# Nine raw buffers, 44 gating column tiles in the first chunk, DMAs on ScalarE's queue, later partial sums

## The chip, the core and the metric

The kernel runs on one core of a Trainium2 chip. The metric is the device time of one execution in microseconds. Before the change three runs took 3028.86 to 3030.75 us, with a median of 3030.44 us.

## What is computed

One layer of a diffusion backbone on a stream of 256 latent tokens with 256 context tokens as a prefix, width D = 4096, all in float32. Cut to what matters:

```python
mod   = silu(c) @ w_ada + b_ada             # shift, scale, gate (4096 each)
mod_c = silu(c_ctx) @ w_ada[:, :2*D] + ...  # shift, scale for the context
h  = rmsnorm(x, g) * (1 + scale) + shift    # 256 x 4096
hc = rmsnorm(ctx, g) * (1 + scale_c) + shift_c
xa, xb, ga, gb = split(h @ w_in)            # 4 x 4096 columns
xa_c = hc @ w_in[:, :4096]
ya = rglru_branch(xa, xa_c, ...)            # conv, gates, scans both ways
yb = pool_branch(xb, w_pool, ...)           # means over windows 2, 4, 8, 16
mixed = concat(ya * silu(ga), yb * silu(gb))
x = x + gate * (mixed @ w_out)
return rmsnorm(x, g_final)
```

The matrices are read once each, and they are most of what is moved: w_ada is 4096 x 12288, w_in 4096 x 16384, w_out 8192 x 4096.

## The kernel before

**Layout.** All activations lie transposed: features on the 128 partitions, tokens along the free axis. A tile of x holds 128 features of the 256 latent and the 256 context tokens (128 x 512), so D is 32 k-tiles. Every weight load is a raw tile of 128 x 1024 float32 (512 KB), taken from the pool of RAWB = 6 buffers and issued by SP (`load_raw`, line 92). `load_w` (line 97) splits it in two parts of lower precision: ACT casts raw to hi (line 101), and lo = raw - hi is made by DVE, or by POOL where the caller asks for it (line 103). The hi pool has 4 buffers, the lo pool 3. A product of float32 values is then three matmuls: hi x hi, hi x lo of the activation, and lo x hi.

**Stages.** In the head (to about 60 us) all 32 x tiles are loaded once for the sum of squares, and the modulation of the first chunk is made. Then comes the chunk stage (to about 900 us): the 32 k-tiles are taken in nine chunks of CHUNKS = (2, 4, 4, 4, 4, 4, 4, 4, 2).

- In chunk c, `xa_units` (line 338) multiplies the xa columns of w_in with the hc tiles of the chunk. A unit is one raw tile, which is two column tiles of 128 for a chunk of four k-tiles: 2 x 4 x 3 = 24 matmuls (lines 351 to 353) of 128 x 512 each, 16 units a chunk. The result of each column tile is in a PSUM tile, of which `mm_tile` has four; ACT copies three of four out to `part` (line 359) and POOL adds them to acc (line 360), DVE adds the fourth (line 362). lo is made by POOL here.
- Beside it, `ada_units` (line 228) makes shift and scale of the next chunk. Its 32 raw tiles of w_ss are not multiplied by PE but by DVE, which adds them up on 128 partitions (line 218); the last addition writes the four tiles fin (line 224). `rows` (line 261) then sums fin over partitions with matmuls against 0/1 columns (line 242; the program has four in the group, the trace counts eight), and `cols` turns the rows into columns (line 197).
- From these `prep_h` (line 301) makes the hc tiles of the next chunk: POOL multiplies x by rstd (line 305), ACT and DVE do the rest. `load_x` (line 317) fetches the x tile again.
- In the first chunk `ahead_units` (line 372) also multiplies the first two k-tiles of AHEAD = 28 of the 48 blocks of two column tiles that the later stage needs (56 column tiles; 12 matmuls of 128 x 256 a block, lines 384 to 386). `spill_ahead` (line 391) writes them to memory, seven a chunk, in chunks 1 to 4. `gated_units` fetches them back and adds them.

From about 900 us to 2300 us the pooling and gate columns follow (`block_units`, lines 618 and 619: 128 x 512 and 128 x 256 matmuls, lo made by DVE), with the scans between them; blocks that were begun ahead start at their third k-tile. The last stage, to 3008 us, is the output product in 16 blocks of 16 units; `out_evac` (line 752) loads the x tile of the residual (xr) when a block ends, adds it, and stores the first ten results to memory (line 775) until the final normalization.

**What sets the order.** The program is a list of events, and each engine runs its instructions in the order of a tile scheduler that takes them from that list. `run` (line 106) issues loads ahead: LOOK = 4 weight tiles and LOOK_A = 2 w_ss or w_gate tiles before their use. `spread` lays one list evenly among another. In chunk c the side list is: the w_ss units of chunk c + 1 that are left, `rows`, `cols`, and the `prep_h` calls; the w_ss units of chunk c + 2 that are already started are put in four pieces by LAGS = (0, 2, 5, 7, 10): two tenths before `rows`, three tenths between `rows` and `cols`, two behind `cols` and three behind three of the prep_h calls. Spills and x loads of the chunk are spread over the first 0.6 of the xa units.

Every DMA carries one of eight semaphores (DMAHW0 to 7), and before it starts it waits until the DMA that last used this semaphore has ended. The wait stands in the program of the engine that issues the DMA, and what follows it on that engine follows the wait.

Of the kernel before, what the change touches and what calls it, by code (L numbers as in the profile page):

```python
# [22 lines left out]
GATE_FROM, GATE_END = 0.9, 0.99  # L23
SPILL_Y = 10
EPS = 1e-6
POOL_ADDS = 3
EARLY = 4
NPREP = 3
LAGS = (0, 2, 5, 7, 10)
LRU_SPAN = 91  # L30
RAWB, HIB, LOB = 6, 4, 3
LOOK = 4
LOOK_A = 2
X_STEP = 2
SHARES = (16, 4, 0, 0, 0, 0, 0, 0, 0)
CHUNKS = (2, 4, 4, 4, 4, 4, 4, 4, 2)
AHEAD = 28
AHEAD_FROM = 48 - AHEAD
SPILLS = 7
W = 1024  # L40
# [25 lines left out]
def block_kernel(ctx, tc, xc, cvec, vecs, consts, w_ss, w_gate, w_xa, w_lat0, w_lat2, w_lat, w_pool, w_rec, w_out, out):  # L66
# [3 lines left out]
    cpool = ctx.enter_context(tc.tile_pool(name="consts", bufs=1))  # L70
    spool = ctx.enter_context(tc.tile_pool(name="slots", bufs=68))
    tpool = ctx.enter_context(tc.tile_pool(name="temps", bufs=14))
# [24 lines left out]
    def load_w(src, eng=None):  # L97
        raw = load_raw(src)
        width = src.shape[-1]
        hi = hip.tile([P, W], F32R, name="hi", tag="hi")[:, :width]  # L100
        act.copy(out=hi, in_=raw)  # L101
        lo = lop.tile([P, W], F32R, name="lo", tag="lo")[:, :width]
        (eng or dve).tensor_tensor(out=lo, in0=raw, in1=hi.bitcast(F32), op=SUB)  # L103
        return hi, lo

    def run(events):
# [194 lines left out]
    def prep_h(k):  # L301
        def f():
            x = xt[k]
            if k >= CHUNKS[0]:
                nc.gpsimd.tensor_tensor(out=x, in0=x, in1=rstd, op=MUL)
            h = mm_tile()
            for v in range(2):
                cut = slice(v * T, (v + 1) * T)
                act.activation(out=h[:, cut], in_=x[:, cut], func=AF.Identity, scale=colA[:, k, v:v + 1],
                               bias=colB[:, k, v:v + 1])  # L310
            hi, lo = temp("hhi", F32R), temp("hlo", F32R)
            split(hi, lo, h)
            hc[k] = (hi, lo)
            xt[k] = None
        return S_(f)

    def load_x(k):
        def f():
            xt[k] = slot("x")
            nc.sync.dma_start(out=xt[k], in_=xc[k])  # L320
        return S_(f)
# [16 lines left out]
    def xa_units(c):  # L338
# [3 lines left out]
        def unit(i):  # L342
            def f(w):
                hi, lo = (t.rearrange("p (k m) -> p k m", k=n) for t in w)
                for j in range(per):
# [26 lines left out]
    def ahead_units():  # L372
        def unit(i):
            def f(w):
                hi, lo = (t.rearrange("p (b k m) -> p b k m", b=2, k=2) for t in w)
                for b in range(2):
# [14 lines left out]
    def spill_ahead(blk):  # L391
        def f():
            nc.sync.dma_start(out=ahead_sp[blk], in_=ahead[blk])
            ahead[blk] = None
# [357 lines left out]
    def out_evac(blk):  # L752
        def f(j, ps):
            ct = 2 * blk + j
            if j == 0:
                xr = temp("xr")
                nc.sync.dma_start(out=xr.rearrange("p (k t) -> p k t", k=2),
                                  in_=xc[ct:ct + 2, :, 0:T].rearrange("k p t -> p k t"))
                ys.append(xr)
            y = ys[blk][:, j * T:(j + 1) * T]  # L760
# [13 lines left out]
            if j == 1 and blk < SPILL_Y:  # L774
                nc.sync.dma_start(out=y_sp[blk], in_=ys[blk])
        return f

    def warm_sqrt():
        t = temp("warm")[:, 0:1]
        act.activation(out=t, in_=ones[:, 0:1], func=AF.Sqrt)  # L780

    events += [make_mix(n) for n in range(4)] + [S_(warm_sqrt)]
    main = [block_units([w_out[blk, i] for i in range(16)], mix, out_evac(blk)) for blk in range(16)]
    pair = [u for two in zip(main[0], main[1]) for u in two]
    main = spread(pair, [make_mix(n) for n in range(4, 32)], 0.0, 28 / 32) + [u for m in main[2:] for u in m]
# [101 lines left out]
```

## Time and profile before

| | |
|---|---|
| median of three runs | 3030.44 us |
| the profiled execution | 3034.39 us, span 3032.6 us |
| mean granted clock of TensorE | 0.985 |
| bytes moved by DMA | 701 MB, 231 GB/s over the span |

The profile is one execution. A line for a stretch gives the busy time of PE (matmul), PEld (weight load), DVE, ACT and POOL, the clock that was granted to TensorE (1.00 is 2.4 GHz, 0.50 is 1.2 GHz) and the use of the 16 DMA engines. A line of waits gives the instruction that waited, what it waited for, the time in all, the number of times and the longest. SPq and ACTq are the queues in which an engine issues its DMAs.

### The profile page before, as it was taken

What the parts mean: (1) busy time and instruction counts of PE and PEld (TensorE: products, weight loads), DVE (VectorE), ACT (ScalarE), POOL (GpSimd) and SP (SyncE); (2) the same over time, 40 slices, a digit from 0 to 9 for tenths busy, and PEclk for the clock granted to TensorE, in tenths of its full rate; (3) what the DMA queues carried; (4) which work ended last, traced back from release to release, by engine and by line L of the source; (5) the groups of instructions that cost most, each with busy time, mean ns of one, the idle gap of its engine ahead of it and who ended that gap; (6) DMA issues with size and microseconds to landing.
All of it is one profiled execution on the core that took longest, in us unless ns stands there. A gap on an engine that the chain in (4) does not pass through costs nothing.

```text
span 3032.6 us, 40790 instructions
## 1 busy us (share of the span) xinstructions
PE 2898.6 (96%) x15032; PEld 2409.5 (79%) x15032; DVE 2232.4 (74%) x2723; ACT 1574.1 (52%) x2183; POOL 590.0 (19%) x348
## 2 busy tenths in 40 slices
PE   6997889899999999999999999999999999999997
PEld 3775667678778888888888888888888888788886
DVE  5787887888656778887777877778997766665445
ACT  4544334334434666766667766767663443333432
POOL 2566677687760000000000000000000000000000
PEclk9998999999999999999999999999999999999998
DMA  8889877788636555555556666666888988786664
GB/s 321 297 289 312 282 256 230 245 283 272 203 103 201 184 161 175 178 175 176 175 184 194 192 193 198 206 202 228 323 291 299 329 288 296 262 296 217 192 190 148
DMA packets 214968, 700.99 MB, mean 231 GB/s; under 512 B 23536, under 2 KB 31856, under 8 KB 214768
## 3 DMA queue, kind: packets, MB, share of 16 engines
q1 hardware_dynamic: 214768, 698.39, 69.7%
q8 instruction: 117, 1.92, 0.3%
q14 instruction: 83, 0.68, 0.1%
HBM read 675.75 MB, written 22.54 MB: 230 GB/s over the span
## 4 chain that ended last, share of the span: by engine, by line
PE 73%; DMA 12%; DVE 9%; issue 3%; POOL 2%; ACT 2%; SPq 0%; DVEq 0%; POOLq 0%; ACTq 0%
PE mm L618 34%; PE mm L619 17%; DMA raw<-in_w_gate 6%; PE mm L351 4%; DVE wide L218 4%; PE mm L352 4%; PE mm L353 4%; DMA raw<-in_w_ss 4%; PE wide L527 2%; PE wide L528 2%; PE wide L529 2%; DVE lo L103 2%; PE mm L242 1%; DMA x<-in_xc 1%; POOL lo L103 1%
## 5 line engine op out<-in xcount | busy, mean ns | idle before, releaser
L101 ACT CAST hi<-raw 128x1024 fp32r<-128x1024 f32 (+1 forms) x846 | 872.0, 1035 | 990.1 <-PE mm L618 539.8
L103 DVE TENSOR_TENSOR lo<-raw,hi 128x1024 fp32r<-128x1024 f32 (+1 forms) x704 | 840.6, 1200 | 369.8 <-PE mm L619 230.3
L618 PE MATMUL mm<-hT,hi 128*128 128x512 f32 x2960 | 1047.2, 398 | 0.0
L218 DVE SCALAR_TENSOR_TENSOR wide<-raw,sc,wide 128x1024 f32<-128x1024 f32 (+1 forms) x592 | 698.5, 1230 | 231.2 <-DMA raw<-in_w_ss 121.5
L619 PE MATMUL mm<-hT,lo 128*128 128x256 f32 x2960 | 831.3, 281 | 0.2 <-DVE lo L103 0.2
L618 PE MATMUL mm<-mix,hi 128*128 128x512 f32 x2048 | 723.8, 398 | 0.0
L618 PEld LDWEIGHTS mm<-hT,hi 128*128 128x128 f32 x2960 | 556.2, 188 | 138.9 <-ACT mix L134 0.9
L619 PE MATMUL mm<-mix,lo 128*128 128x256 f32 x2048 | 578.0, 282 | 13.4 <-DVE lo L103 13.2
L619 PEld LDWEIGHTS mm<-hT,lo 128*128 128x128 f32 x2960 | 559.1, 189 | 1.8 <-DVE lo L103 0.5
L618 PEld LDWEIGHTS mm<-mix,hi 128*128 128x128 f32 x2048 | 385.2, 188 | 94.6 <-ACT hi L101 1.7
L351 PE MATMUL mm<-hhi,hi 128*128 128x512 f32 x1024 | 403.1, 395 | 16.7 <-ACT hhi L134 7.4
L352 PE MATMUL mm<-hlo,hi 128*128 128x512 f32 x1024 | 401.0, 392 | 4.9 <-DVE hlo L135 4.9
L619 PEld LDWEIGHTS mm<-mix,lo 128*128 128x128 f32 x2048 | 387.4, 189 | 22.1 <-DVE lo L103 21.8
L353 PE MATMUL mm<-hhi,lo 128*128 128x512 f32 x1024 | 400.2, 391 | 0.0
L103 POOL TENSOR_TENSOR lo<-raw,hi 128x1024 fp32r<-128x1024 f32 x142 | 340.7, 2400 | 192.2 <-ACT hi L101 61.0
L351 PEld LDWEIGHTS mm<-hhi,hi 128*128 128x128 f32 x1024 | 193.0, 189 | 70.1 <-DVE acc L362 9.9
L360 POOL TENSOR_TENSOR acc<-acc,part 128x512 f32<-128x512 f32 x168 | 215.4, 1293 | 114.2 <-ACT part L359 114.0
L352 PEld LDWEIGHTS mm<-hlo,hi 128*128 128x128 f32 x1024 | 193.3, 189 | 46.9 <-DVE hlo L135 7.7
L353 PEld LDWEIGHTS mm<-hhi,lo 128*128 128x128 f32 x1024 | 193.2, 189 | 40.6
L359 ACT COPY part<-mm 128x512 f32<-128x512 f32 x168 | 96.5, 584 | 128.1 <-PE mm L353 117.2
L527 PE MATMUL wide<-uhi,hi 128*128 128x512 f32 x256 | 101.1, 395 | 3.3 <-ACT i L541 2.2
L528 PE MATMUL wide<-ulo,hi 128*128 128x512 f32 x256 | 100.4, 392 | 0.0
(140 smaller groups left out, 2331.9 us busy)
## 6 DMA issues: line engine op xcount, KB each, us to landing
raw<-in_w_lat SPq DMA_DIRECT2D x370, 512.0 KB, 3.7
raw<-in_w_ss SPq DMA_DIRECT2D x256, 512.0 KB, 4.9
raw<-in_w_out SPq DMA_DIRECT2D x256, 512.0 KB, 4.5
raw<-in_w_xa SPq DMA_DIRECT2D x128, 512.0 KB, 4.5
raw<-in_w_gate SPq DMA_DIRECT2D x128, 512.0 KB, 4.9
raw<-in_w_rec SPq DMA_DIRECT2D x32, 512.0 KB, 3.7
raw<-in_w_pool SPq DMA_DIRECT2D x32, 512.0 KB, 3.7
x<-in_xc SPq DMA_DIRECT2D x58, 256.0 KB, 6.6
```

Source lines behind the costliest of these rows:

```text
L101: act.copy(out=hi, in_=raw)
L103: (eng or dve).tensor_tensor(out=lo, in0=raw, in1=hi.bitcast(F32), op=SUB)
L218: dve.scalar_tensor_tensor(out=accs[v][:, :width], in0=seg, scalar=s, in1=accs[v][:, :width], op0=MUL, op1=ADD)
L351: pe.matmul(out=ps, lhsT=wh, rhs=a, start=(k == 0), stop=False)
L352: pe.matmul(out=ps, lhsT=wh, rhs=b, start=False, stop=False)
L353: pe.matmul(out=ps, lhsT=wl, rhs=a, start=False, stop=(k == n - 1))
L359: act.copy(out=part, in_=ps)
L360: nc.gpsimd.tensor_tensor(out=acc[o], in0=acc[o], in1=part, op=ADD)
L527: pe.matmul(out=o, lhsT=wh[:, g, k, m], rhs=st["hi"][k], start=(k == 0), stop=False)
L528: pe.matmul(out=o, lhsT=wh[:, g, k, m], rhs=st["lo"][k], start=False, stop=False)
L618: pe.matmul(out=ps, lhsT=hi[:, k, m], rhs=a, start=first, stop=False)
L619: pe.matmul(out=ps[:, 0:T], lhsT=lo[:, k, m], rhs=a[:, 0:T], start=False, stop=last)
```

## The change

RAWB is 9, LOOK 5 and LOOK_A 4, and the pool of slots is 62 tiles where it was 68, which makes the room: three raw buffers are six slots. AHEAD is 22, so 44 column tiles are begun in the first chunk where it was 56, and SPILLS is 6. LAGS becomes (0, 4, 6, 8, 10): four tenths of the w_ss units of the chunk after next stand ahead of `rows`, and `rows` that much later among the xa units. x tiles, the spills and the stores y_sp are issued by ACT. POOL's multiplication of x by rstd is made to come behind the lo in use (`issue_after`). The fetch of xr is an event of its own, four units before a block ends.

```diff
-LAGS = (0, 2, 5, 7, 10)
+LAGS = (0, 4, 6, 8, 10)
-RAWB, HIB, LOB = 6, 4, 3
-LOOK = 4
-LOOK_A = 2
+RAWB, HIB, LOB = 9, 4, 3
+LOOK = 5
+LOOK_A = 4
-AHEAD = 28
+AHEAD = 22
-SPILLS = 7
+SPILLS = 6
+FETCH_X = 12
...
-    spool = ctx.enter_context(tc.tile_pool(name="slots", bufs=68))
+    spool = ctx.enter_context(tc.tile_pool(name="slots", bufs=62))
...
-        (eng or dve).tensor_tensor(out=lo, in0=raw, in1=hi.bitcast(F32), op=SUB)
+        ins = (eng or dve).tensor_tensor(out=lo, in0=raw, in1=hi.bitcast(F32), op=SUB)
+        if eng is not None:
+            lo_ins.append(ins)
...
-                nc.gpsimd.tensor_tensor(out=x, in0=x, in1=rstd, op=MUL)
+                with tc.issue_after(lo_ins[used[0] - 1].ins):
+                    nc.gpsimd.tensor_tensor(out=x, in0=x, in1=rstd, op=MUL)
...
             xt[k] = slot("x")
-            nc.sync.dma_start(out=xt[k], in_=xc[k])
+            act.dma_start(out=xt[k], in_=xc[k])
...
     def spill_ahead(blk):
         def f():
-            nc.sync.dma_start(out=ahead_sp[blk], in_=ahead[blk])
+            act.dma_start(out=ahead_sp[blk], in_=ahead[blk])
...
     def out_evac(blk):
-            if j == 0:
-                xr = temp("xr")
-                nc.sync.dma_start(out=xr.rearrange("p (k t) -> p k t", k=2),
-                                  in_=xc[ct:ct + 2, :, 0:T].rearrange("k p t -> p k t"))
-                ys.append(xr)
...
             if j == 1 and blk < SPILL_Y:
-                nc.sync.dma_start(out=y_sp[blk], in_=ys[blk])
+                act.dma_start(out=y_sp[blk], in_=ys[blk])
...
+    def fetch_x(blk):
+        def f():
+            xr = temp("xr")
+            nc.sync.dma_start(out=xr.rearrange("p (k t) -> p k t", k=2),
+                              in_=xc[2 * blk:2 * blk + 2, :, 0:T].rearrange("k p t -> p k t"))
+            ys.append(xr)
+        return S_(f)
...
+    for blk in range(16):
+        main[blk].insert(FETCH_X, fetch_x(blk))
```

`used` counts the xa and ahead units that have been reached; the names `lo_ins` and `used` serve `issue_after` alone. Line numbers of the changed kernel are 5 to 8 higher in the chunk stage: line 242 becomes 247, 351 to 353 become 358 to 360, 393 becomes 401.

**PE, the group of line 242 in chunk 2** (fin: DVE's sums for the chunk after; mm: PSUM; hhi, hlo, hi, lo: the halves of hc and of the weights; in brackets the engines whose semaphore the instruction waits for). Before:

```order
L351 MATMUL mm_2835<-hhi_2409,hi_2608 128x512
L352 MATMUL mm_2835<-hlo_2410,hi_2608 128x512
L353 MATMUL mm_2835<-hhi_2409,lo_2610 128x512
L242 MATMUL mm_2868<-fin_2853,cst_81 4x512 [waits DVE_49,Activation_49]
L242 MATMUL mm_2868<-fin_2857,cst_81 4x512 [waits DVE_49]
L242 MATMUL mm_2868<-fin_2855,cst_81 4x512
L242 MATMUL mm_2868<-fin_2859,cst_81 4x512 [waits DVE_49]
L351 MATMUL mm_2881<-hhi_2251,hi_2659 128x512
L352 MATMUL mm_2881<-hlo_2252,hi_2659 128x512
L353 MATMUL mm_2881<-hhi_2251,lo_2661 128x512 [waits Pool_49]
```

and now, with the lines 247 and 358 to 360:

```order
L358 MATMUL mm_2772<-hhi_2292,hi_2495 128x512
L359 MATMUL mm_2772<-hlo_2293,hi_2495 128x512
L360 MATMUL mm_2772<-hhi_2292,lo_2497 128x512
L247 MATMUL mm_2796<-fin_2735,cst_81 4x512 [waits DVE_49,Activation_49]
L358 MATMUL mm_2809<-hhi_2174,hi_2546 128x512 [waits Activation_49]
L359 MATMUL mm_2809<-hlo_2175,hi_2546 128x512
L360 MATMUL mm_2809<-hhi_2174,lo_2548 128x512 [waits Pool_49]
L247 MATMUL mm_2796<-fin_2739,cst_81 4x512 [waits DVE_49]
L247 MATMUL mm_2796<-fin_2737,cst_81 4x512
L247 MATMUL mm_2796<-fin_2741,cst_81 4x512 [waits DVE_49]
L358 MATMUL mm_2809<-hhi_2220,hi_2546 128x512
L359 MATMUL mm_2809<-hlo_2221,hi_2546 128x512
```

Before, the first matmul of the group stands behind 9 of the chunk's 16 units of 24 matmuls; now it stands behind 10, and three matmuls of the next unit stand before the other three. Counted in the same way over chunks 1 to 7, the group stood behind 10, 9, 9, 9, 11, 12 and 13 units, and now behind 11, 10, 10, 11, 12, 12 and 13.

**ACT, the middle of the first chunk** (ahead: an ahead tile in a slot, copied there from PSUM in four pieces; ahead_131: its place in memory). Before:

```order
L101 CAST hi<-raw 128x1024 [waits DMAHW1_49,PE_49,Pool_49]
L387 COPY ahead<-mm 128x256 [waits PE_49] x4
L101 CAST hi<-raw 128x1024 [waits DMAHW4_49,PE_49,Pool_49]
L387 COPY ahead<-mm 128x256 [waits PE_49]
L356 COPY acc<-mm 128x512 [waits PE_49] x3
L101 CAST hi<-raw 128x1024 [waits DMAHW7_49,PE_49,Pool_49]
L356 COPY acc<-mm 128x512 [waits PE_49]
L387 COPY ahead<-mm 128x256 [waits PE_49] x3
L101 CAST hi<-raw 128x1024 [waits DMAHW2_49,PE_49,Pool_49]
L387 COPY ahead<-mm 128x256 [waits PE_49] x5
L101 CAST hi<-raw 128x1024 [waits DMAHW5_49,Pool_49]
```

and now:

```order
L102 CAST hi<-raw 128x1024 [waits DMAHW0_49,PE_49,Pool_49]
L395 COPY ahead<-mm 128x256 [waits PE_49]
L401 DMA ahead_130<-ahead 128x512 [waits DMAHW4_49,Activation_49]
L363 COPY acc<-mm 128x512 [waits PE_49] x3
L102 CAST hi<-raw 128x1024 [waits DMAHW7_49,PE_49,Pool_49]
L363 COPY acc<-mm 128x512 [waits PE_49]
L395 COPY ahead<-mm 128x256 [waits PE_49] x2
L401 DMA ahead_131<-ahead 128x512 [waits DMAHW0_49,Activation_49]
L395 COPY ahead<-mm 128x256 [waits PE_49]
L102 CAST hi<-raw 128x1024 [waits DMAHW3_49,PE_49,Pool_49]
L395 COPY ahead<-mm 128x256 [waits PE_49]
L401 DMA ahead_132<-ahead 128x512 [waits Activation_49]
```

A spill stands right behind the second copy of its block, ahead of the casts and copies of the next one, and waits for a DMA semaphore like the casts do. 20 of the 22 spills stand in this chunk, the other two and eight x loads at the start of chunk 1; in each later chunk the four x loads stand among ACT's casts.

**SP, the start of chunk 1.** Before:

```order
L94 DMA raw<-in_w_ss 128x1024 [waits DMAHW4_49,DVE_49]
L94 DMA raw<-in_w_ss 128x1024 [waits DMAHW5_49,DVE_49]
L94 DMA raw<-in_w_xa 128x1024 [waits DMAHW3_49,Pool_49]
L393 DMA ahead_129<-ahead 128x512
L393 DMA ahead_130<-ahead 128x512
L94 DMA raw<-in_w_ss 128x1024 [waits DMAHW6_49,DMAHW1_49,DVE_49]
L94 DMA raw<-in_w_ss 128x1024 [waits DMAHW7_49,Pool_49]
L94 DMA raw<-in_w_ss 128x1024 [waits DMAHW2_49,DMAHW0_49,DVE_49]
L393 DMA ahead_131<-ahead 128x512
L94 DMA raw<-in_w_xa 128x1024 [waits Pool_49]
L94 DMA raw<-in_w_ss 128x1024 [waits DMAHW6_49,DMAHW3_49,DVE_49]
L320 DMA x<-in_xc 128x512 [waits DMAHW4_49]
```

and now:

```order
L95 DMA raw<-in_w_xa 128x1024 [waits DMAHW7_49,DMAHW2_49,DVE_49]
L95 DMA raw<-in_w_ss 128x1024 [waits DMAHW0_49,Pool_49]
L95 DMA raw<-in_w_xa 128x1024 [waits DMAHW1_49,DVE_49]
L95 DMA raw<-in_w_ss 128x1024 [waits DMAHW3_49,DVE_49]
L95 DMA raw<-in_w_xa 128x1024 [waits DMAHW4_49,DVE_49]
L95 DMA raw<-in_w_ss 128x1024 [waits DMAHW6_49,DVE_49]
L95 DMA raw<-in_w_xa 128x1024 [waits DMAHW7_49,Pool_49]
L95 DMA raw<-in_w_ss 128x1024 [waits DMAHW0_49,DVE_49]
L95 DMA raw<-in_w_ss 128x1024 [waits DMAHW5_49,DMAHW1_49,Pool_49]
L95 DMA raw<-in_w_ss 128x1024 [waits DMAHW2_49,DVE_49]
L95 DMA raw<-in_w_xa 128x1024 [waits DMAHW4_49,Pool_49]
```

SP has nothing but raw loads there now. Spills and x loads are gone from its queue, and a raw load waits for the engine that last read the buffer nine loads before it, where it was six.

## Rows read from the trace of the kernel before

**Rows 1.** Page, part 1: busy time, share of the span, instructions
```profile
PE 2898.6 (96%) x15032; PEld 2409.5 (79%) x15032; DVE 2232.4 (74%) x2723; ACT 1574.1 (52%) x2183; POOL 590.0 (19%) x348
```

**Rows 2.** Busy time by stage: stretch, its length, busy us (x instructions), PEclk, DMA share, GB/s
```profile
148.44:244.10 95.66, 80.51 (x362) 61.83 (x361) 84.64 (x79) 38.80 (x70) 58.25 (x34) 0.93 0.83 291
...
470.00:575.00 105.00, 93.46 (x395) 72.19 (x393) 84.77 (x79) 38.03 (x60) 72.21 (x45) 0.95 0.75 247
575.00:680.00 105.00, 103.49 (x448) 81.98 (x447) 85.37 (x82) 42.43 (x67) 82.05 (x49) 1.00 0.77 259
...
1000.00:2300.00 1300.00, 1289.67 (x7068) 1108.76 (x7067) 1027.86 (x1464) 867.02 (x1179) 0.00 (x0) 1.00 0.63 202
...
3008.50:3032.60 24.10, 3.66 (x17) 2.23 (x15) 15.02 (x25) 2.76 (x7) 0.00 (x0) 0.65 0.51 174
```

**Rows 3.** Timeline of PE, line 242: start, us, form, [idle before <- releaser]
```profile
241.67 6.42 PE L242 MATMUL mm<-fin,cst 128*4 128x512 f32 x8 [12.03 <-DVE fin L224]
...
345.67 5.63 PE L242 MATMUL mm<-fin,cst 128*4 128x512 f32 x8 [8.78 <-DVE fin L224]
...
451.98 5.38 PE L242 MATMUL mm<-fin,cst 128*4 128x512 f32 x8 [9.53 <-DVE fin L224]
...
558.62 4.97 PE L242 MATMUL mm<-fin,cst 128*4 128x512 f32 x8 [9.56 <-DVE fin L224]
...
764.62 3.60 PE L242 MATMUL mm<-fin,cst 128*4 128x512 f32 x8
```

**Rows 4.** Busy time in steps of 2 us around the first wait
```profile
236.00:238.00 2.00, 0.00 (x0) 0.00 (x0) 2.00 (x2) 0.00 (x0) 0.00 (x0) 0.50 1.17 342
...
246.00:248.00 2.00, 2.00 (x4) 0.15 (x2) 2.00 (x3) 1.11 (x2) 0.00 (x0) 0.65 0.97 296
248.00:250.00 2.00, 2.00 (x10) 1.65 (x10) 1.76 (x2) 0.89 (x2) 0.31 (x1) 1.00 0.94 306
```

**Rows 5.** Timeline of PE: matmuls of one xa and one ahead tile
```profile
663.84 0.39 PE L351 MATMUL mm<-hhi,hi 128*128 128x512 f32 x1
...
664.52 0.39 PE L351 MATMUL mm<-hhi,hi 128*128 128x512 f32 x1
...
71.59 0.28 PE L384 MATMUL mm<-hhi,hi 128*128 128x256 f32 x1
...
72.31 0.28 PE L384 MATMUL mm<-hhi,hi 128*128 128x256 f32 x1
```

**Rows 6.** Who waited: DVE, 60 to 244 us; all engines, 150 to 660 us
```profile
DVE wide L218 <- DMA raw<-in_w_ss: 25.4, 16, 5.1
...
DVE wide L218 <- DMA raw<-in_w_ss: 73.6, 53, 6.2
```

**Rows 7.** SP's queue, 150 to 660 us: what its DMA issues waited for
```profile
SPq L94 <- POOL lo L103: 187.4, 65, 6.4
SPq L94 <- DVE wide L218: 169.8, 111, 2.7
```

**Rows 8.** Busy time by stage, columns as in rows 2
```profile
60.11:148.44 88.33, 81.40 (x443) 66.09 (x444) 69.33 (x61) 49.56 (x95) 46.05 (x22) 0.94 0.81 282
...
244.10:347.50 103.40, 91.08 (x377) 70.23 (x376) 84.57 (x81) 38.94 (x61) 75.78 (x47) 0.93 0.92 310
```

**Rows 9.** DMA issues of line 393: duration of the issue, then time to landing
```profile
L393 SPq DMA_DIRECT2D ahead<-ahead x28: 326/424/1848, 165.5 to 345.3; - x28
...
DMA to landing us min/median/max: 4.4/6.0/8.6
```

**Rows 10.** Who waited, 150 to 660 us; and for tile xr, whole span
```profile
POOL x L305 <- DMA x<-in_xc: 17.9, 8, 7.8
...
  DMA xr<-in_xc: 0.6, 1
```

**Rows 11.** Who waited: PE, 2300 to 2960 us
```profile
PE mm L619 <- DVE lo L103: 13.2, 17, 2.2
```

**Rows 12.** Who waited, all engines, 150 to 660 us
```profile
ACT hi L101 <- DMA raw<-in_w_xa: 121.6, 27, 7.5
```

More of the change, by code (lines that the diff above doesn't have):

```diff
@@ L102, in load_w @@
         lo = lop.tile([P, W], F32R, name="lo", tag="lo")[:, :width]
-        (eng or dve).tensor_tensor(out=lo, in0=raw, in1=hi.bitcast(F32), op=SUB)
+        ins = (eng or dve).tensor_tensor(out=lo, in0=raw, in1=hi.bitcast(F32), op=SUB)
+        if eng is not None:
+            lo_ins.append(ins)
         return hi, lo
+    lo_ins, used = [], [0]
     def run(events):
@@ L343, in f @@
             def f(w):
+                used[0] += 1
                 hi, lo = (t.rearrange("p (k m) -> p k m", k=n) for t in w)
@@ L374, in f @@
             def f(w):
+                used[0] += 1
                 hi, lo = (t.rearrange("p (b k m) -> p b k m", b=2, k=2) for t in w)
```

## Prediction

> **What bounds the kernel now.** I read the page's shares first, then the busy time by stage, then who waits for whom inside the chunk stage, and last the few microseconds around one wait. PE is busy for 96% of the span [rows 1]. From 1000 us on it is the bound without doubt: 1289.67 of 1300 us, 7068 matmuls, 0.1825 us each [rows 2]. What ends the run after the last matmul, 24.1 us from 3008.5 us, is not touched. The chunk stage (about 62 to 900 us) is different: from 148.44 to 244.10 us PE works 80.51 of 95.66 us, in 470 to 575 us 93.46 of 105, and only from 575 us on is it full (103.49 of 105) [rows 2]. So time can be won there, and nearly only there.
>
> The lost time has one shape. Once per chunk PE multiplies the partial sums that DVE accumulated (tile fin, line 242), and in four chunks it stands before that: 12.03, 8.78, 9.53 and 9.56 us, 39.9 together [rows 3]. It costs more than the wait. During it the granted clock falls to 0.50, the 1.2 GHz level, and is back at 1.00 only at 248 us [rows 4], so the eight matmuls that follow take 6.42, 5.63, 5.38 and 4.97 us where the group at 764.62 us, with no wait before it, takes 3.60 [rows 3]: 22.40 - 4 x 3.60 = 8.0 us. The waits are worth 47.9 us.
>
> Why is fin late? A matmul of the xa work starts every 0.2267 us (three in 0.68 us), so one of the 16 column units of a chunk, 24 matmuls, is 5.4 us of PE [rows 5]. Counted in PE's order, the group of line 242 stands behind 10, 9, 9 and 9 units in the four chunks that wait, and behind 11, 12 and 13 in the three that don't. Place decides. And DVE, which makes fin, stands still itself: for 25.4 us between 60 and 244 us, and for 73.6 us between 150 and 660, waiting for w_ss transfers [rows 6]. Those come late because SP's queue waits for a free raw buffer, 187.4 us for POOL's lo and 169.8 us for DVE [rows 7].
>
> **The change, part by part.**
>
> *Later sums, nine raw buffers, longer look-ahead.* These go together. In the new PE order the four groups stand behind 11, 10, 10 and 11 units, that is one unit (5.4 us) later in the first three and two in the fourth. By place alone 12.0 - 5.4 = 6.6, 3.4, 4.1 and 0 us of wait stay: 14.1. Three more buffers let SP load three transfers further, so DVE's own waiting goes down as well. For the first group there is a floor: DVE is busy 69.33 + 84.64 = 154 us from 60.11 us until fin is written at 244.1 [rows 2, 8], so without a single wait fin would be there at 214 us. With half of its 25.4 us gone and the rest of its idle time kept I put it near 230, where PE would arrive at about 224: 6 us of wait stay, plus 1 us of low clock. From then on DVE needs 84.77 us a chunk [rows 2] and PE 16 x 5.4 + 3.6 + small groups, about 93, so DVE gains on PE and the other three waits go. Term: -47.9 + 7 = **-41 us**. Ends: -47.9, and -30 (14.1 us of wait and half of the 8.0 stay).
>
> *44 column tiles ahead instead of 56.* Six blocks of 12 matmuls leave the first chunk: 72 matmuls at 0.12 us (six in 0.72 us [rows 5]), 8.6 us. The same blocks later take 48 more matmuls in the stage from 1000 us: 48 x 0.1825 = 8.8 us, all on the path. What the first chunk gives back depends on who bounds it. PE is busy 81.40 of 88.33 us there, DVE 69.33 [rows 8], but the spills now fall into it too (22 x 256 KB, against three 512 KB transfers less), and its end hangs on fin. I count 3 of the 8.6 us: **+6 us**; ends 0 and +9. The six reloads and twelve adds that go lie beside other work.
>
> *x tiles and spills by ScalarE's queue.* 26 x loads, 22 spills and 10 stores of y are 58 issues. One costs 0.424 us on SP [rows 9]; at that price it is 25 us of an engine that is about half busy, hidden by its idle time; if the cover were gone it would be 25 us on the path. What SP gains is not on the path either: POOL waited 17.9 us for x tiles [rows 10], but PE never waited for POOL. The Trainium skill (DMA: Bandwidth & Descriptors, Issuing engines are not separate DMA queues) says that a second issuing engine only saves the sequencer time of the issue; by that rule this part is worth 0, while a reading in which POOL's wait was on the path would give -18. The trace agrees with the 0: SP's large waits are for buffers [rows 7].
> The cost is the waiting. Each of these DMAs waits for the DMA that last used its semaphore (eight are dealt round), and with that wait in ACT's program all copies and casts behind it wait, so PE's four PSUM tiles fill. Free to PE: four tiles, 4 x 12 x 0.2267 = 10.9 us in a four-k chunk, 4 x 0.72 = 2.9 us in a run of ahead tiles. In the new order most of the 22 spills in and after the first chunk wait for a DMA that is about as old as the raw tile that ACT has cast last, so it has landed. Bounds: 0, and 62 us (rival 4). I take **+3 us**, near the lower end, because that landing is what the cast itself waited for.
>
> *POOL's x multiplies set behind the lo in use, residual x fetched four units earlier.* The first frees POOL's order, which PE did not wait for. The second removes at most the 0.6 us that DVE waited for xr [rows 10]. Both 0.
>
> *62 slots instead of 68.* In the new SP order eight of the ten y reloads wait until the last output block frees mix tiles. That block lasts 256 x 0.1825 = 47 us, and such a 256 KB load lands in about 6 us [rows 9]: 0.
>
> *Output stage.* PE waits 13.2 us for lo while DVE is held by gate transfers [rows 11]. Deeper buffers should take about half, as I assumed for DVE's waits above: **-6 us**; ends 0 and -13.2.
>
> Sum: -41 + 6 + 3 - 6 = -38 us. The profiled execution took 3034.4 us (span 3032.6), 4 above the median of the runs; against the median 3030.4 that gives **2992 us**.
>
> **Rivals.**
> 1. *DVE stays the late one.* The deeper buffers do not bring w_ss sooner, since all loads share one stream that already reaches 310 GB/s between 244.1 and 347.5 us [rows 8]; then only the place helps and term one is -30: 3003 us. For it: DVE has no idle time to spare just before 244 us. Against: between 470 and 575 us it idles 20 us.
> 2. *Everything hides.* All four waits with their clock (47.9), all lo waits (13.2), the ahead tiles in balance: -61, 2969 us. Against: the floor of the first group.
> 3. *ACT is held by x loads in six chunks.* They stand in groups of up to four, and the last waits for a transfer six places behind the last one cast: 6 x 2.1 us (105 us for some 50 transfers) + 6.0 us to land [rows 9] - 10.9 us of cover = 7.7 us, six times, 46 us, in place of my +3: 3035 us, no change. For it: ACT already waits up to 7.5 us for an xa transfer [rows 12]. Against: with full buffers the six are already there.
> 4. *Slower: the spills hold ACT in the first chunk.* A spill lands in 6.0 us [rows 9]; if each of 20 spills waits that long, less 2.9 us of cover, it is 3.1 x 20 = 62 us: -38 - 3 + 62 = +21, 3051 us. It decides where the DMA before it on its semaphore is itself a spill or a load that SP has not issued yet. For it: five of the 20 follow another spill. Against: that spill is mostly a whole unit older. The Trainium skill (TensorE: Matmul & The Clock Gate, the paragraph on engine queue depths) calls ScalarE a strict FIFO, and by that rule this is how ACT behaves; the trace agrees as far as ACT's 7.5 us of idling shows it.
>
> **Chances.** My forecast 0.56, rival 1 0.20, rival 2 0.10, rival 3 0.06, rival 4 0.08. A measurement of this kernel can tell about 0.2% (6 us) from no change. Forecast and rivals 1 and 2 are faster: 0.86; rival 3 is the same: 0.06; rival 4 is slower: 0.08. The range takes in rivals 1 and 2 and, above, the partial holds of ACT up to 30 us: 2966 to 3022.
>
> **What would show it.** Right: PE's wait for fin under 10 us in all, and the granted clock at 0.98 or more from 260 to 575 us; those line 242 groups about 93 to 97 us apart instead of 104 to 107; SP's waits for lo and for DVE and DVE's waits for w_ss clearly smaller; the stage from 1000 to 2300 us at the same 0.1825 us a matmul. Wrong: waits of ACT for spills or x loads above some 10 us in sum with PE waiting for acc, part or ahead tiles (rivals 3, 4); DVE full and PE still waiting about 14 us for fin (rival 1).

## The result and the profile after

Four runs of the changed kernel took 2959.65 to 2964.52 us, with a median of 2962.36; the kernel before, timed beside it, 3030.60. The ratio is 0.9775, with a 95% interval of 0.9758 to 0.9792: 68 us faster. The forecast was 2992 us (2966 to 3022); the measured time lies below the range. The profiled span fell from 3032.6 to 2961.1 us, by 71.5.

The page's first part of the kernel after:

```profile
PE 2885.2 (97%) x15008; PEld 2408.5 (81%) x15008; DVE 2231.2 (75%) x2711; ACT 1573.8 (53%) x2168; POOL 584.8 (20%) x345
```

PE did 24 matmuls less, was busy for 13.4 us less and stood still for 58.1 us less. Where, the stages tell. Of the kernel after, busy time (columns as in rows 2) of the first chunk up to the partial-sum group that ends it, of the next three intervals between such groups, of all seven together, and of the output stage:

```profile
60.00:138.15 78.15, 76.04 (x401) 60.27 (x401) 70.36 (x62) 45.16 (x83) 37.16 (x16) 0.96 0.93 350
...
138.15:226.01 87.86, 82.08 (x353) 63.57 (x353) 82.18 (x78) 39.53 (x69) 56.93 (x32) 0.94 0.91 337
226.01:315.08 89.07, 88.44 (x376) 69.10 (x377) 81.38 (x78) 37.42 (x59) 69.96 (x44) 0.98 0.78 274
315.08:408.20 93.12, 92.66 (x401) 73.25 (x401) 88.58 (x85) 38.48 (x61) 73.18 (x44) 1.00 0.83 292
...
138.15:794.00 655.85, 648.31 (x2801) 513.16 (x2800) 561.02 (x564) 276.27 (x434) 509.79 (x303) 0.99 0.77 273
2193.50:2938.60 745.10, 736.21 (x4135) 633.13 (x4134) 467.71 (x487) 309.02 (x375) 0.00 (x0) 1.00 0.76 253
```

and of the kernel before the first, the seven together, and the output stage:

```profile
60.00:150.38 90.38, 83.34 (x449) 66.53 (x450) 70.74 (x63) 50.11 (x97) 47.65 (x23) 0.95 0.81 281
150.38:862.10 711.72, 658.95 (x2826) 516.23 (x2824) 562.90 (x564) 278.71 (x444) 506.54 (x302) 0.96 0.77 259
2258.00:3009.90 751.90, 738.52 (x4135) 631.59 (x4134) 466.02 (x481) 304.31 (x363) 0.00 (x0) 1.00 0.76 253
```

| stretch | before | after | difference | forecast |
|---|---|---|---|---|
| 60 us to the first group of line 242 / 247 | 90.4 | 78.2 | -12.2 | -3 |
| that group to the last of its kind | 711.7 | 655.9 | -55.9 | -38 |
| from there to the first matmul on hT | 68.2 | 66.9 | -1.3 | 0 |
| matmuls on hT (line 618 / 626), first to last | 1327.8 | 1332.6 | +4.8 | +8.8 |
| output stage | 751.9 | 745.1 | -6.8 | -6 |

(The +6 for the ahead tiles was -3 in the first chunk and +8.8 for the 48 later matmuls; -38 is -41 with the +3 for ACT.) The first two rows are not bounded by the same work: of the 72 ahead matmuls that left the first chunk, 48 stood before the first group and 24 behind it (PE's counts, 449 to 401 and, with one at the edge, 2826 to 2801). At 0.12 us each [rows 5] that is 5.8 us of the first row and 2.9 of the second. In the second row PE's idle time, the stretch less its busy time, fell from 52.8 to 7.5 us, and its busy time by 10.6 with those matmuls gone and at a clock of 0.99 where it was 0.96.

The same groups as in [rows 3], in the timeline of PE after:

```profile
226.01 5.29 PE L247 MATMUL mm<-fin,cst 128*4 128x512 f32 x8 [2.10 <-ACT part L366]
...
315.08 1.02 PE L247 MATMUL mm<-fin,cst 128*4 128x512 f32 x2 [0.63 <-DVE fin L229]
...
316.93 2.74 PE L247 MATMUL mm<-fin,cst 128*4 128x512 f32 x6
...
408.20 3.60 PE L247 MATMUL mm<-fin,cst 128*4 128x512 f32 x8
...
506.42 3.60 PE L247 MATMUL mm<-fin,cst 128*4 128x512 f32 x8
```

The third line belongs to the second group, which is broken by three other matmuls. DVE's work on fin before the first line's group:

```profile
221.79 2.72 DVE L229 SCALAR_TENSOR_TENSOR fin<-raw,sc,wide 128x512 f32<-128x512 f32 x4
```

From 408 us on there is no wait and no low clock: 3.60 us each. From the first to the last of the seven intervals the groups are 88 to 98 us apart.

Why is fin in time? Of the kernel after, who waited: first DVE from 60 to 226 us, then all engines from 150 to 660 us, then SP's queue in that stretch, as in [rows 6], [rows 12] and [rows 7]:

```profile
DVE wide L223 <- DMA raw<-in_w_ss: 3.5, 5, 1.4
DVE wide L221 <- DMA raw<-in_w_ss: 3.4, 1, 3.4
```

```profile
ACT hi L102 <- DMA raw<-in_w_xa: 8.9, 2, 5.0
...
DVE wide L223 <- DMA raw<-in_w_ss: 0.7, 2, 0.4
```

```profile
SPq L95 <- POOL lo L104: 290.8, 87, 6.8
SPq L95 <- DVE wide L223: 97.7, 105, 3.5
```

DVE's waits for w_ss fell from 25.4 to 6.9 us in the first stretch and from 73.6 to 0.7 in the second, and ACT's for w_xa from 121.6 to 8.9. SP's own waits for a free buffer did not shrink: 357 us before [rows 7], 388 after. With buffers that are all full the wait of the queue is only the sign that it is ahead; the same number with starved engines meant that it was late.

PE's waits in the chunk stage besides those for fin, before (60 to 900 us) and after (60 to 840 us):

```profile
PE mm L352 <- DVE hlo L135: 4.9, 5, 1.8
PE mm L384 <- ACT ahead L387: 4.0, 5, 1.3
PE mm L351 <- DVE acc L362: 4.0, 5, 1.4
PE mm L384 <- ACT acc L356: 3.8, 2, 3.3
PE mm L351 <- DVE hlo L135: 3.1, 1, 3.1
```

```profile
PE mm L358 <- ACT hhi L139: 8.9, 2, 7.4
PE mm L358 <- DVE acc L369: 3.0, 3, 2.0
...
PE mm L359 <- DVE hlo L140: 1.5, 4, 0.5
PE mm L358 <- ACT ahead L395: 1.3, 1, 1.3
```

The 7.4 us on hhi stand in both kernels, at the start of the stage. Without them these waits were 20.2 us in sum before and are 8.9 after.

### The profile page after: what moved, and what is told of

It reads as the page before. It is cut to its first block, busy times and chain, and to the rows that moved or that the text cites. A ratio compares the mean times of both kernels' runs of the same rounds, so it can differ in the third digit from the quotient of the medians.

```text
span 2961.1 us, 40678 instructions
## 1 busy us (share of the span) xinstructions
PE 2885.2 (97%) x15008; PEld 2408.5 (81%) x15008; DVE 2231.2 (75%) x2711; ACT 1573.8 (53%) x2168; POOL 584.8 (20%) x345
## 4 chain that ended last, share of the span: by engine, by line
PE 87%; DMA 7%; DVE 4%; issue 1%; ACT 1%; POOL 0%; SPq 0%; DVEq 0%; ACTq 0%
PE mm L626 38%; PE mm L627 19%; PE mm L358 7%; PE mm L359 7%; PE mm L360 7%; DMA raw<-in_w_gate 4%; PE wide L535 2%; PE wide L536 2%; PE wide L537 2%; DVE wide L223 2%; PE mm L247 1%; DMA x<-in_xc 1%; DMA raw<-in_w_ss 1%; DVE lo L104 1%; PE mm L202 0%
## 5 line engine op out<-in xcount | busy, mean ns | idle before, releaser
L102 ACT CAST hi<-raw 128x1024 fp32r<-128x1024 f32 x843 | 873.3, 1039 | 917.9 <-PE mm L626 586.0
L104 POOL TENSOR_TENSOR lo<-raw,hi 128x1024 fp32r<-128x1024 f32 x139 | 334.3, 2406 | 191.1 <-POOL acc L367 62.6
L369 DVE TENSOR_TENSOR acc<-mm,acc 128x512 f32<-128x512 f32 x88 | 60.1, 687 | 78.2 <-PE mm L360 77.9
```

The costliest lines, as they stand in the source:

```text
L104: ins = (eng or dve).tensor_tensor(out=lo, in0=raw, in1=hi.bitcast(F32), op=SUB)
L369: dve.tensor_tensor(out=acc[o], in0=ps, in1=acc[o], op=ADD)
```

## The experiments

Every kernel was timed beside the kernel before on its own chip; from chip to chip the median of the kernel before lay between 3030.0 and 3034.6 us. e4 and e6 do one part of the change on the kernel before; the others start from the changed kernel.

| kernel | us, median (lowest to highest) | ratio to before, interval |
|---|---|---|
| e1, LAGS back | 2968.89 (2965.99 to 2972.48) | 0.9797 (0.9780 to 0.9813) |
| e2, six raw buffers | 3002.87 (2999.52 to 3004.10) | 0.9905 (0.9891 to 0.9920) |
| e3, DMAs back on SP | 2956.61 (2953.95 to 2958.63) | 0.9754 (0.9739 to 0.9769) |
| e4, before with LAGS | 3005.30 (3001.61 to 3008.97) | 0.9915 (0.9898 to 0.9932) |
| e6, before with nine buffers | 2967.51 (2966.26 to 2970.29) | 0.9790 (0.9776 to 0.9805) |
| e7, no issue_after | 2966.68 (2961.16 to 2969.53) | 0.9780 (0.9764 to 0.9797) |
| e8, 28 blocks ahead | 2959.57 (2955.67 to 2963.74) | 0.9763 (0.9747 to 0.9779) |
| e9, ten buffers, SP | 2959.85 (2958.76 to 2962.53) | 0.9765 (0.9751 to 0.9780) |
| e10, x loads on SP | 2965.08 (2964.70 to 2965.65) | 0.9787 (0.9772 to 0.9801) |
| e11, spills on SP | 2960.52 (2958.45 to 2963.98) | 0.9773 (0.9758 to 0.9787) |
| e12, e3 with 28 blocks | 2954.31 (2951.65 to 2957.28) | 0.9751 (0.9737 to 0.9766) |
| e13, LOOK as before | 2963.06 (2961.79 to 2964.75) | 0.9782 (0.9765 to 0.9798) |
| e14, the changed kernel again | 2963.21 (2958.32 to 2967.56) | 0.9771 (0.9752 to 0.9791) |
| e15, xr as before | 2969.35 (2967.80 to 2970.79) | 0.9792 (0.9775 to 0.9809) |
| e16, e3 again | 2956.47 (2955.28 to 2958.83) | 0.9750 (0.9733 to 0.9767) |
| e17, e12 again | 2955.87 (2953.30 to 2961.73) | 0.9752 (0.9733 to 0.9770) |

### Buffers or place (e1, e2, e4, e6)

e1, the changed kernel with the old LAGS:

```diff
-LAGS = (0, 4, 6, 8, 10)
+LAGS = (0, 2, 5, 7, 10)
```

> The changed kernel with LAGS back at (0, 2, 5, 7, 10), all else kept; the partial-sum group then stands behind 10, 10, 10 and 10 units in chunks 1 to 4 instead of 11, 10, 10 and 11. Theory depth (nine raw buffers keep DVE supplied, so the sums are early enough anywhere): 0 to +7 us against the changed kernel's 2962, at most the first group waits one unit longer. Theory place (the later position of the group is what won): two groups one unit (5.4 us) earlier, with the low clock behind the waits +13 to +20 us.

e2, the changed kernel with the old number of buffers:

```diff
-RAWB, HIB, LOB = 9, 4, 3
-LOOK = 5
-LOOK_A = 4
+RAWB, HIB, LOB = 6, 4, 3
+LOOK = 4
+LOOK_A = 2
```

> The changed kernel with 6 raw buffers, LOOK 4 and LOOK_A 2 as before, all else kept (44 ahead tiles, 62 slots, later sums, ScalarE's queue); the groups stay behind 11, 10, 10 and 11 units. Theory depth: +40 to +55 us (3002 to 3017), DVE waits over 50 us for w_ss between 140 and 640 us again and PE waits for fin again. Theory place: +5 to +15 us, PE waits for fin under 15 us in all.

e4, the kernel before with the new LAGS:

```diff
-LAGS = (0, 2, 5, 7, 10)
+LAGS = (0, 4, 6, 8, 10)
```

> The kernel before with LAGS (0, 4, 6, 8, 10) alone; the group stands behind 11, 10, 10 and 10 units instead of 10, 9, 9 and 9. Theory place: each of the four waits gets 5.4 us shorter and the low clock shorter with it, -22 to -30 us against 3030. Theory depth: DVE is as badly supplied as before and PE only waits later: 0 to -22 us, with DVE's waits for w_ss still above 60 us between 150 and 660 us.

e6, the kernel before with the buffers and what makes their room:

```diff
-RAWB, HIB, LOB = 6, 4, 3
-LOOK = 4
-LOOK_A = 2
+RAWB, HIB, LOB = 9, 4, 3
+LOOK = 5
+LOOK_A = 4
-AHEAD = 28
+AHEAD = 22
-SPILLS = 7
+SPILLS = 6
-    spool = ctx.enter_context(tc.tile_pool(name="slots", bufs=68))
+    spool = ctx.enter_context(tc.tile_pool(name="slots", bufs=62))
```

> The kernel before with nine raw buffers, LOOK 5, LOOK_A 4, and what makes their room (62 slots, 44 ahead tiles); LAGS, queues, POOL's order and xr as before. The group stands behind 10 units in chunks 1 to 4. Theory depth alone: it gives nearly all that the sums' later place and it give together: 2965 to 2975 us, with DVE's waits for w_ss under 5 us between 150 and 660 us. If depth and place were additive (40 of depth as measured in e2_raw6): about 2990 us.

Place alone gave -25 us (e4), buffers alone -63 (e6), the whole change -68. e6 has the 44 ahead tiles and the look-ahead beside its buffers, but these are worth nothing that the runs can tell (e8 and e13 below). So the two overlap: beside six buffers the place is worth 25 us, as theory place had it and more than theory depth allowed (DVE's waits for w_ss are 45.9 us in e4, where theory depth had over 60); beside nine it is worth some 6.5 (e1 against 2962.36, on another chip and with intervals that overlap), as theory depth had it. 4.4 of them stand at the group of chunk 1, which in e1 waits 5.30 us for fin and takes 6.52, where it was 2.10 and 5.29. Taking only the buffers from the changed kernel cost 40.5 us (e2), the lower end of what theory depth named, though DVE waited only 38.3 us for w_ss between 150 and 660 us and not over 50. Theory place falls by e1, e2 and e6. Who waited in e6, from 150 to 660 us:

```profile
ACT hi L101 <- DMA raw<-in_w_xa: 8.3, 2, 5.6
...
PE mm L242 <- DVE fin L224: 7.8, 1, 7.8
...
DVE wide L218 <- DMA raw<-in_w_ss: 7.0, 8, 1.7
```

DVE's 73.6 us of before are 7.0 (a little above the 5 expected), ACT's 121.6 are 8.3, and of the four waits for fin one of 7.8 us is left, the first. What e2 lost again is for the most part not those waits: its groups wait 13.2 us in all against 2.7, and the other waits of PE are back (60 to 870 us):

```profile
PE mm L359 <- DVE hlo L140: 4.5, 3, 2.1
PE mm L358 <- ACT ahead L395: 4.2, 2, 2.9
PE mm L358 <- DVE hlo L140: 3.6, 2, 2.2
PE mm L358 <- DVE acc L369: 3.4, 4, 2.0
PE mm L392 <- ACT acc L363: 3.1, 1, 3.1
PE mm L358 <- ACT part L366: 3.1, 2, 2.5
```

With two smaller ones these are 25.2 us, where the changed kernel has 8.9.

Six buffers held not only DVE. Of e2, PE's group of line 247 in chunk 1, DVE's fin before it, and ACT around it (timelines of PE, DVE and ACT):

```profile
246.03 5.79 PE L247 MATMUL mm<-fin,cst 128*4 128x512 f32 x8 [9.71 <-ACT part L366]
```

```profile
237.52 2.72 DVE L229 SCALAR_TENSOR_TENSOR fin<-raw,sc,wide 128x512 f32<-128x512 f32 x4
```

```profile
236.02 1.05 ACT L102 CAST hi<-raw 128x1024 fp32r<-128x1024 f32 x1 [7.10 <-DMA raw<-in_w_xa]
244.45 1.04 ACT L102 CAST hi<-raw 128x1024 fp32r<-128x1024 f32 x1 [7.38 <-DMA raw<-in_w_xa]
245.40 1.06 ACT L366 COPY part<-mm 128x512 f32<-128x512 f32 x2
```

The wait is put down to ACT. fin is complete at 240.24 us, and yet the group starts at 246.03: it needs a PSUM tile, two copies of `part` that would free one stand in ACT's order behind a cast, and this cast waits for its w_xa transfer until 244.45. In e4, where no DMA is in ACT's program, it is the same: fin done at 240.0, group at 245.89. The prediction cited the Trainium skill (TensorE: Matmul & The Clock Gate, the paragraph on engine queue depths) for ScalarE being a strict FIFO; these rows agree with it, with a late weight transfer as the thing that blocks. The changed kernel has a small case of it: fin is complete at 224.51 us, and the group starts at 226.01, behind a copy that follows a cast which waited 4.96 us for w_xa.

### Look-ahead, and a tenth buffer (e13, e9)

e13, the changed kernel with the old look-ahead, nine buffers kept:

```diff
-LOOK = 5
-LOOK_A = 4
+LOOK = 4
+LOOK_A = 2
```

> The changed kernel with LOOK 4 and LOOK_A 2 as before, nine raw buffers kept. Theory buffers (SP runs ahead by as many loads as there are buffers, whatever the order of the list): 2962 within 5 us. Theory look-ahead (two w_ss tiles in flight are too few for DVE): 2980 to 3003 us, DVE waits over 20 us for w_ss.

2963.06 us, no difference from 2962.36: it is the buffers, not the look-ahead. e9, e3 with one more:

```diff
-RAWB, HIB, LOB = 9, 4, 3
-LOOK_A = 4
+RAWB, HIB, LOB = 10, 4, 3
+LOOK_A = 5
-    spool = ctx.enter_context(tc.tile_pool(name="slots", bufs=62))
+    spool = ctx.enter_context(tc.tile_pool(name="slots", bufs=60))
```

> The changed kernel with all x loads, spills and y stores on SP (as e3_sp_queue, 2957 us), ten raw buffers, LOOK_A 5 and 60 slots. If supply still limits: 2 to 6 us faster than e3_sp_queue. If nine buffers are enough: 2957 within 3 us, since DVE's waits for w_ss are already gone.

2959.85 us, not faster than e3. Nine are enough here.

### 44 or 56 column tiles ahead (e8)

```diff
-AHEAD = 22
+AHEAD = 28
-SPILLS = 6
+SPILLS = 7
```

> The changed kernel with 28 blocks (56 column tiles) ahead and 7 spills a chunk again, 62 slots kept: 72 matmuls more in the first chunk, 48 fewer later. Theory PE-bound first chunk (with full raw buffers all of the 8.6 us shows there): the first chunk 8 to 9 us longer, the stage after the chunks 8 to 9 us shorter, in sum 0 within 4 us. The prediction's view (3 of the 8.6 us show): 4 to 7 us faster than the changed kernel.

The first chunk of e8 up to the group:

```profile
60.00:147.61 87.61, 85.74 (x473) 69.37 (x473) 75.74 (x66) 52.24 (x99) 45.67 (x21) 0.95 0.93 362
```

87.61 us against 78.15: 9.5 us for the 72 matmuls, which are 8.6 us at 0.12. With full buffers the first chunk pays for all of them. The matmuls on hT took 1327.7 us, 4.9 less than in the changed kernel, and not the 8 to 9 that was expected. Another 3.8 us came back at the group of chunk 1, which in e8 starts without a wait and takes 3.60 us, where it was 2.10 and 5.29. The time, 2959.57, is 2.8 us lower, less than the runs can tell; the two costs balance in sum, as the theory of a PE-bound first chunk had it. The prediction's view would have asked for 4 to 7.

### POOL's order and xr (e7, e15)

e7:

```diff
-                with tc.issue_after(lo_ins[used[0] - 1].ins):
-                    nc.gpsimd.tensor_tensor(out=x, in0=x, in1=rstd, op=MUL)
+                nc.gpsimd.tensor_tensor(out=x, in0=x, in1=rstd, op=MUL)
```

> The changed kernel without the issue_after on POOL's x multiplications, all else kept. Prediction's view (PE does not wait for POOL's x): 2962 within 3 us. Rival (an x multiplication ahead of a lo makes PE wait for that lo): +4 us or more, with PE's waits for lo in the chunk stage above 2 us.

2966.68 us, 4.3 above the changed kernel, with ranges that overlap (2961.16 to 2969.53, and 2959.65 to 2964.52; 2958.32 to 2967.56 in e14): whether it is slower is not settled. PE waited for no lo in the chunk stage in either kernel, so the rival's mechanism did not show. e15, the load of xr moved back into `out_evac` and `fetch_x` taken out:

```diff
         def f(j, ps):
             ct = 2 * blk + j
+            if j == 0:
+                xr = temp("xr")
+                nc.sync.dma_start(out=xr.rearrange("p (k t) -> p k t", k=2),
+                                  in_=xc[ct:ct + 2, :, 0:T].rearrange("k p t -> p k t"))
+                ys.append(xr)
...
-    for blk in range(16):
-        main[blk].insert(FETCH_X, fetch_x(blk))
```

> The changed kernel with the residual x loaded when a block ends, as before; all else kept. Theory buffers (the nine raw buffers shorten the output stage): output stage 744.5 within 2 us, time within 2 us of e14_after_again. Theory fetch (the early fetch does): output stage 749 to 752 us, 5 to 7 us slower than e14_after_again.

6.1 us slower than e14, of which the output stage has 3.1 (747.3 against 744.2 us from its first to its last matmul), less than theory fetch said and more than theory buffers did. Of the rest 2.5 us are there already at the first group of line 247 (141.5 against 139.0 us), where nothing was changed, so they can't be put down to xr. On the same measure the kernel before has 751.3, e6 (buffers, old xr) 746.3 and e2 (six buffers, early xr) 744.6. So beside six buffers the early xr goes with 6.7 us and beside nine with 3.1, and the buffers with the old xr go with 5.0 (e2 and e6 hold other parts of the change too). Either part alone gives most of the 6.8 us, and how they share it is open.

### ScalarE's queue (e3, e10, e11, e16, e14)

e3 and e16:

```diff
-            act.dma_start(out=xt[k], in_=xc[k])
+            nc.sync.dma_start(out=xt[k], in_=xc[k])
...
-            act.dma_start(out=ahead_sp[blk], in_=ahead[blk])
+            nc.sync.dma_start(out=ahead_sp[blk], in_=ahead[blk])
...
-                act.dma_start(out=y_sp[blk], in_=ys[blk])
+                nc.sync.dma_start(out=y_sp[blk], in_=ys[blk])
```

> The changed kernel with x tiles, spills and y stores issued by SP again, all else kept. Theory queue (the spills and x loads in SP's order held the raw loads behind them): +10 to +30 us, DVE's waits for w_ss back above 20 us. Theory depth: 0 to +5 us, since nine buffers cover a raw load that is issued a few us later. If the DMA waits in ACT's program cost something, it is faster: -1 to -5 us.

e10 has the first of these edits alone, e11 the second.

> The changed kernel with the 26 x loads alone back on SP; spills and y stores stay on ACT. Theory issue time (ACT is busy without a gap from 152 to 162 us of the changed kernel, and eight x loads of 0.34 to 0.6 us each stand in and right behind this stretch): it wins most of what e3_sp_queue won, 2956 to 2959 us. Theory spills (the DMA waits of the spills in the first chunk are what costs): 2961 to 2964 us.

> The changed kernel with the 22 spills alone back on SP; x loads and y stores stay on ACT. Theory issue time of the x loads: 2960 to 2963 us, little won. Theory spills: 2956 to 2959 us, the first chunk 1 to 2 us shorter than in the changed kernel.

e14 is the changed kernel, without an edit.

> The changed kernel itself, as the common base of the other three of this call: 2962 within 3 us, the first group of line 247 in the chunks at 138 us, output stage (first to last matmul on mix) 744.5 us within 2.

> x loads, spills and y stores on SP (e3_sp_queue once more), beside e14_after_again on the same chip. If ACT's queue costs what e3_sp_queue showed: 4 to 7 us faster than e14_after_again. If that was the difference between two chips: within 2 us of it.

On one chip e16 took 2956.47 us and e14 2963.21, with ranges that overlap by 0.5 us, and e3 had shown 5.8: the three kinds of DMA on ACT's queue cost some 6 us. Theory queue falls, since it had SP's order as the cost. Where the spills are issued decides when they run. Line 401 of e14 and of e16 (duration of the issue in ns, first and last start), and the stretch from 100 to 140 us of each, in that order:

```profile
L401 ACTq DMA_DIRECT2D ahead<-ahead x22: 326/326/352, 71.2 to 178.6; - x22
```

```profile
100.00:140.00 40.00, 37.71 (x207) 28.91 (x206) 33.51 (x31) 21.82 (x41) 20.85 (x10) 1.00 0.96 361
```

```profile
L401 SPq DMA_DIRECT2D ahead<-ahead x22: 326/424/1467, 151.6 to 351.7; - x22
```

```profile
100.00:140.00 40.00, 39.99 (x213) 29.58 (x212) 37.57 (x34) 23.38 (x43) 22.20 (x10) 1.00 0.93 336
```

By ACT the spills run from 71 us on, beside the raw loads of the first chunk, and the DMA engines are full (share 0.96, 361 GB/s; in the profile of the changed kernel 1.01 and 381). DVE works 33.51 of 40 us. By SP they wait until 151 us, and DVE works 37.57. The other kernels with nine buffers and 22 spills divide in the same way: with the spills by ACT DVE works 33.5 to 35.9 us in this stretch (the changed kernel, e1, e7, e10, e13, e14, e15), with the spills by SP 37.3 to 37.7 (e3, e6, e11, e16). In e16 DVE completes fin at 222.35 us, and PE waits 0.2 us for it, where it waits 2.1 to 2.4 behind ACT's copies in the changed kernel:

```profile
219.64 2.71 DVE L229 SCALAR_TENSOR_TENSOR fin<-raw,sc,wide 128x512 f32<-128x512 f32 x4
```

```profile
221.75 2.74 PE L247 MATMUL mm<-fin,cst 128*4 128x512 f32 x6 [0.21 <-DVE fin L229]
```

Of the 7.5 us that e16 is ahead of e14 at the first matmul on hT, 1.1 are there at the group that ends the first chunk and 4.9 at the group of chunk 1. The Trainium skill (DMA: Bandwidth & Descriptors, Issuing engines are not separate DMA queues) says that such transfers share the same 16 engines; these rows agree, with 22 transfers more beside the weights and less work for DVE. What the section gives as the gain of a second issuing engine, the time of the issue, was not to be seen here.

Neither edit alone gave it. e11 brought fin to 221.33 us, but PE then waited until 225.14. ACT in e11 (timeline):

```profile
217.65 1.05 ACT L102 CAST hi<-raw 128x1024 fp32r<-128x1024 f32 x1 [7.51 <-DMA raw<-in_w_xa]
219.46 0.33 ACTq L326 DMA_DIRECT2D x<-in_xc  x1
223.56 1.04 ACT L102 CAST hi<-raw 128x1024 fp32r<-128x1024 f32 x1 [4.85 <-DMA raw<-in_w_xa]
224.51 1.07 ACT L366 COPY part<-mm 128x512 f32<-128x512 f32 x2
```

The copies at 224.51 stand behind a cast that waited 4.85 us for w_xa, with an x load between it and the cast before. The changed kernel has nearly the same wait there (4.96 us) and no x load, so the x load is not what holds it. In e16 a copy of part stands ahead of the cast that follows (at 219.40 us); moving the DMAs also changed ACT's order, and no run parts the two. And in e11 the x loads that stayed with ACT do what rival 3 feared, on a small scale: a cast, a copy of rows and a copy of part behind them wait 3.5, 5.1 and 2.9 us for a spill or a weight transfer that holds the semaphore, though no wait of PE is put down to them. e10 was not faster than the changed kernel at all, so theory issue time falls, and theory spills was half right: the first chunk got 1 us shorter, as it said, and the time 1.8 us. That the early spills feed DVE worse is shown; that this is what costs the 6 us is not, since the spills alone gave less than the runs can tell. How the 6 us divide among the three kinds of DMA stays open.

### The fastest (e12, e17)

e3 with AHEAD = 28 and SPILLS = 7.

> e3_sp_queue (2957 us) with 28 blocks ahead and 7 spills a chunk as before, 62 slots. By e8_ahead28, where the first chunk got 9.5 us longer and the rest 9 to 12 us shorter: 2954 to 2959 us, that is no difference that can be told from e3_sp_queue. If SP's spills hold raw loads in the first chunks: over 2962 us.

> The same with 28 blocks ahead (e12_sp_ahead28 once more). Theory balance (what the first chunk pays, the later stage gives back): within 3 us of e16_sp_queue_again, and so 2 to 9 us faster than e14_after_again.

2954.31 and 2955.87 us: faster than the kernel before by 2.5% and than the changed kernel by 7 us on the same chip (e17 against e14; the slowest run of e17 lies above the two fastest of e14). From e16 it can't be told.

## Why the prediction was wrong

The direction and the largest term were right: the four waits went. But the sum has no term for what the buffers did besides, and that is more than half of the miss. By the profiled spans the forecast of -38 came as -71.5. Of the 33 us between them, 19 lie in PE's other stalls of the chunk stage and its clock, 6 in the ahead tiles of the first chunk, 4 in the matmuls on hT, 2 in the four groups and 2 in the rest.

- **The step that failed: PE's other stalls in the chunk stage, which the sum leaves at nothing.** The prediction let the deeper buffers act on the groups alone, and took "half of its 25.4 us gone" for DVE. Three more buffers took away nearly all waits for transfers of DVE (73.6 to 0.7) and of ACT (121.6 to 8.9). For the groups that mattered little, since they could not win more than 47.9. It mattered for PE's stalls on hlo, acc, the ahead tiles and ACT's copies, each too short to be given a price: 20.2 us before, 8.9 after, and 25.2 in e2, where six buffers are back. In the stage table the first two rows together won 68.1 us; less the groups (43.3) and the 72 ahead matmuls (8.7) that leaves 16, of which 13 are idle time and 3 busy time at the higher clock. The sum has +3 in that place, for ACT. ACT's 121.6 us were in [rows 12], used there for a rival only; in e2 they are what stands behind PE's longest wait.
- **The four waits and their clock.** Forecast -41 of 47.9 us. Measured: waits of 39.9 became 2.10 + 0.63, and the group's own time is 5.29 in the first, 3.76 in the two pieces of the second and 3.60 in the third and fourth. About -43. The reason was right in part: the prediction gave the place 25.8 of the 39.9 us of wait, and "Place decides" does not hold, since with nine buffers and the old place one wait is left (e6). That the first of the four has a floor held: fin was complete at 224.5 us, between the 214 without a wait and the 230 that I took. PE came at 223.9, beside the 224 that was named, and that was luck: from the 229.6 at which PE stood before, the prediction's own 5.4 for the place and 3 for the ahead tiles make 232. The ahead tiles, which came back whole, and the stalls that went brought PE forward instead.
- **44 tiles.** Forecast: 3 of 8.6 us come back in the first chunk. e8 shows all of it, 9.5 us. The reason given for the 3, that the end of the chunk hangs on fin, is not in the rows: neither kernel waits for fin at the group that ends the first chunk (150.38 us before, 138.15 after).
- **x tiles and spills by ScalarE.** Forecast +3, bounds 0 and 62. Measured about +6 (e3, e16), with the sign right. The waits on DMA semaphores, on which +3 and rivals 3 and 4 were built, are not what the rows show: before its 22 spills ACT stands still for 0.4 us in all in the changed kernel (4.0 in e14), before its x loads not at all. What they show is that the earlier spills take DMA time from the first chunk's weights; that this makes up the 6 us is not shown.
- **Output stage.** Forecast -6 by the buffers, measured -6.8, in part by luck: PE's waits for lo fell by 4.6 us (13.2 to 8.6), and the early xr, which I had costed at 0, gives about 3 beside nine buffers (e15).
- **Later matmuls.** Forecast +8.8 on the path, measured +4.8 for the stage: the 8.8 less about 4 us, of which 3.1 are waits of the gates' matmuls (line 527: 3.3 us before, 0.2 after).
- **The signs to look for.** PE's wait for fin under 10 us and the clock of 0.98 to 1.00 came true, and so did groups 93 to 98 us apart from 315 us on. The later matmuls kept their pace (0.1826 us each from 920 to 2190 us). That SP's waits get smaller did not: those for DVE fell (169.8 to 97.7), those for lo grew (187.4 to 290.8), and the sum by 31 us; of themselves they mean nothing.

The measured 2962 us lies beside rival 2 (2969 us, everything hides), to which I gave 0.10 against the floor of the first group. The floor was real, but it concerned one group. Rival 2 came near by terms that cancel: it had no price for the short stalls either, and it counted more than came for the groups (47.9 against 43) and for the output stage (13.2 against 6.8).

## What to carry to other kernels

Where several engines feed from one rolling set of buffers, a shallow set starves them all together: price every wait on a transfer in the stage, and the short stalls behind them, not only the one long wait that the profile names. A long wait of the issuing queue tells nothing by itself; whether it is late is read at the engines that use the transfers. A deeper pool and a later use both cure one late tile, so their gains overlap and must not be added: alone they gave 63 and 25 us here, together with all else 68.

## What was not expected

A wait that is put down to ACT's PSUM copy was a late weight transfer two steps away (e2: 5.8 of the 9.71 us came after fin was complete). And moving transfers to another engine's queue changed when they ran, 22 spills of 256 KB from 71 us on instead of 151, and with it how much DVE could work beside them; neither the time of issuing them nor, in the changed kernel, the waits on semaphores showed as a cost.
